# Weights-stationary products as three 256-column matmuls in one PSUM half instead of 512 + 256 columns joined afterwards

## Chip, cores, metric

One core of one Trainium2 chip. The metric is device time of one execution in microseconds, median of the runs.

## What is computed

Four post-norm residual layers on x of 256 tokens x 2048 features, float32: gated linear attention (GLA), a gated ConvFFN, a 2-D neighbourhood attention with relative position bias, and a second ConvFFN.

```python
def reference(x, ...):
    for i in range(DEPTH):                     # DEPTH = 2
        m = _gla_mixer(x, ...) if i % 2 == 0 else _na_mixer(x, ...)
        x = _layer_norm(DEEPNORM_ALPHA * x + m, ...)
        f = _conv_ffn(x, ffn_w_up[i], ffn_conv_w[i], ffn_conv_b[i], ffn_w_down[i])
        x = _layer_norm(DEEPNORM_ALPHA * x + f, ...)
    return x

def _conv_ffn(x, w_up, conv_w, conv_b, w_down):
    h = x @ w_up                               # 2048 -> 2 x 5632
    hp = jnp.pad(h, ((0, 0), (1, 1), (0, 0)))
    h = hp[:, :-2] * conv_w[0] + hp[:, 1:-1] * conv_w[1] + hp[:, 2:] * conv_w[2] + conv_b
    a, b = jnp.split(h, 2, axis=-1)
    return (jax.nn.gelu(a, approximate=False) * b) @ w_down
```

GLA projects x to q, k (1024 columns each), v, a gate g (2048 each) and a low-rank decay gate; the attention projects to q, k, v of 2048 each, 16 heads of 128.

## The kernel before

**Precision.** Every float32 operand is split into a high part (rounded to the type fp32r) and a low part, the rest (`emit_split`, lines 129 to 131: a ScalarE cast, a VectorE subtraction). A product is hi·hi + hi·lo + lo·hi. The activations xT and gT lie transposed in SBUF as tiles of 128 features with axes (k tile, token half t, part h, 128 tokens), where h = 0 is the high part and h = 1 the low one.

**Weights.** They come from HBM in units of 128 x 2048 floats (1 MB), in the order of `unit_plan`. `pump` (line 133) loads three units ahead (`raw`, DMA from the SyncE queue) and splits up to NS = 4 units ahead of the one in use into `hi` and `lo`, two pieces of 1024 columns each. `take` gives the next unit, `finish` frees one and calls `pump`.

**Two ways to multiply.** `as_block` (line 218) keeps activations stationary and streams 512 weight columns, for v, g and all output and down projections: three matmuls per k tile and token half. The weights-stationary way is used for q and k of GLA (16 units), q and k of the attention (32 units) and the up-projections (168 units), 216 units in all: `ws_one` (line 203) takes a unit of 128 output features, 16 k tiles, and `ws_part` (line 195) does two matmuls for each,

```python
mm(ps, hi3[:, kc], xs[:, kc].rearrange("p t h n -> p (t h n)"), kc == 0, False)
mm(ps4[:, :, 0], lo3[:, kc], xs[:, kc, :, 0], False, kc == KC - 1)
```

the first streams both parts of x (512 columns: for each token half 128 of the high part, then 128 of the low part) into a whole PSUM bank, the second streams the high parts alone (256 columns) with the low weights. The bank then holds two sums, of which the one over low parts has to be added: `join` (line 498) copies the odd quarter blocks to SBUF on ScalarE (line 502) and adds on VectorE (line 503). Each matmul has its own weight load of 128 columns. The first three units are done by the start-up code, which calls `ws_part` itself for three units side by side (line 449), and `low_rank` (line 480) has its own copy of the two lines.

**After the join.** In GLA the result goes to q or k. In the attention `qk_out` (line 747) splits it once more. In the FFN `conv` (line 673) multiplies by the middle tap and adds the bias on GpSimd (line 684), adds the two outer taps on VectorE (lines 685, 686), then comes Gelu on ScalarE (697) for the first half, or the product (702) and a split into gT for the second. Eight pieces of the FFN come from transposes instead and take the branch `joined`, whose middle tap is a ScalarE activation that reads PSUM (line 682).

**Order.** Work off the main line (scores, softmax, layer norms) is queued with `later` and let in by `tick` between groups of four k tiles. Each engine runs its own instructions in order. PSUM has five banks for `ps_mm` and three for `ps_tp`.

Of the kernel before, what the change touches and what calls it, by code (L numbers as in the profile page):

```python
# [10 lines left out]
F32 = mybir.dt.float32  # L11
F32R = mybir.dt.float32r
I32 = mybir.dt.int32
AF = mybir.ActivationFunctionType
ALU = mybir.AluOpType
AX = mybir.AxisListType

P = 128
D = 2048
T = 256  # L20
KC = D // P
# [16 lines left out]
NCT = FF // P  # L38
# [38 lines left out]
def kernel(  # L77
# [16 lines left out]
    nc = tc.nc  # L94
# [14 lines left out]
    def ps_mm():  # L109
        return psum.tile([P, 512], F32, tag="mm", name="ps_mm", bufs=8 - TP)  # L110

    def ps_tp():
        return psum.tile([P, 512], F32, tag="tp", name="ps_tp", bufs=TP)
# [15 lines left out]
    def emit_split(src, hi, lo):  # L129
        nc.scalar.copy(hi, src)  # L130
        nc.vector.tensor_tensor(lo, src, hi.bitcast(F32), ALU.subtract)  # L131
# [27 lines left out]
    def take():  # L159

        pump()
        j = st["next"]
        st["next"] = j + 1
        return splits.pop(j)

    def finish():
        st["done"] += 1
        pump()
# [3 lines left out]
    def later(fn, delay=1, chain=True):  # L172

        now = st["tick"]
        due = delay + (max([now] + [d for d, _ in side[-1:]]) if chain else now)
        side.append((due, fn))
        side.sort(key=lambda i: i[0])

    def tick():
        st["tick"] += 1  # L180
        while side and side[0][0] <= st["tick"]:
            side.pop(0)[1]()

        if slow and slow[0][0] <= st["tick"]:
            slow.pop(0)[1]()
# [5 lines left out]
    def mm(o, l, r, start, stop):  # L191
        nc.tensor.matmul(o, l, r, start=start, stop=stop)  # L192


    def ws_part(xs, hi, lo, ps, kcs):
        hi3 = hi.rearrange("p (k m) -> p k m", m=P)
        lo3 = lo.rearrange("p (k m) -> p k m", m=P)
        ps4 = ps.rearrange("p (t h n) -> p t h n", t=2, h=2)
        for kc in kcs:
            mm(ps, hi3[:, kc], xs[:, kc].rearrange("p t h n -> p (t h n)"), kc == 0, False)  # L200
            mm(ps4[:, :, 0], lo3[:, kc], xs[:, kc, :, 0], False, kc == KC - 1)

    def ws_one(xs, evac):
        hi, lo = take()
        ps = ps_mm()
        for c in range(4):
            ws_part(xs, hi, lo, ps, range(4 * c, 4 * c + 4))
            tick()
        evac(ps)
        finish()  # L210

# [57 lines left out]
    xT = act.tile([P, KC, 2, 2, P], F32R, tag="xT", name="xT")  # L269
# [87 lines left out]
    def load_g(pool, idx):  # L357
        g = pool.tile([P, D], F32, tag="gb", name="g")
        nc.gpsimd.dma_start(g, lnp[idx, 0:1, :].broadcast_to([P, D]))
        return g  # L360

    def load_gb(pool, idx):
        b = pool.tile([P, D], F32, tag="b", name="b")
        nc.gpsimd.dma_start(b, lnp[idx, 1:2, :].broadcast_to([P, D]))
        return load_g(scope["xp"], idx), b
# [32 lines left out]
    def open_pool(name):  # L398
        scope["pool"] = scope["stack"].enter_context(tc.tile_pool(name=name, bufs=1))
        return scope["pool"]  # L400
# [7 lines left out]
    gla = open_pool("gla")  # L408
# [43 lines left out]
    hi = hi_p.tile([P, 2048], F32R, tag="hi", name="hi")  # L452
    lo = lo_p.tile([P, 2048], F32R, tag="lo", name="lo")
# [44 lines left out]
    def join(pool, dst, ps):  # L498

        ps4 = ps.rearrange("p (t h n) -> p t h n", t=2, h=2)  # L500
        tmp = pool.tile([P, 2, P], F32, tag="join", name="join_t", bufs=2)
        nc.scalar.copy(tmp, ps4[:, :, 1])  # L502
        nc.vector.tensor_tensor(dst.rearrange("p (t n) -> p t n", t=2), ps4[:, :, 0], tmp, ALU.add)  # L503

    def gla_head(h):
        q = gla.tile([P, 2, T], F32, tag="q", name="q")
        k = gla.tile([P, 2, T], F32, tag="k", name="k")
# [122 lines left out]
        if h == 0:  # L630
            for c in range(2):
                join(gla, q[:, c], first_ps[c])
                finish()
            join(gla, k[:, 0], first_ps[2])
            finish()
            ws_one(xT, lambda ps: join(gla, k[:, 1], ps))
            low_rank()
        later(gate_weights, 0)
        later(lambda: gates(0), 4 if h == 0 else 2)
        later(lambda: gates(1), 3)  # L640
        if h > 0:
            for c in range(2):
                ws_one(xT, lambda ps: join(gla, q[:, c], ps))
            for c in range(2):
                ws_one(xT, lambda ps: join(gla, k[:, c], ps))
        later(lambda: decay(0), 1)
        later(lambda: decay(1), 4)
        later(scores, 6)
# [16 lines left out]
    def ffn(layer):  # L665
        pool = scope["pool"]
        idx = 2 * layer + 1
        cw = pool.tile([P, 2 * NCT, 3], F32, name="cw")
        nc.gpsimd.dma_start(cw, convw[:, layer])
        cb = pool.tile([P, 2 * NCT], F32, name="cb")  # L670
        nc.gpsimd.dma_start(cb, convb[:, layer])

        def conv(i, ch, ps, joined=False):
            if joined:
                hh = ps
            else:
                hh = pool.tile([P, T], F32, tag="h", name="h", bufs=3)
                join(pool, hh, ps)
            c = pool.tile([P, T], F32, tag=f"c{i}", name="c", bufs=2)
            w_ = cw[:, ch]  # L680
            if joined:
                nc.scalar.activation(c, hh, AF.Identity, bias=cb[:, ch:ch + 1], scale=w_[:, 1:2])
            else:
                nc.gpsimd.tensor_scalar(c, hh, w_[:, 1:2], cb[:, ch:ch + 1], ALU.mult, ALU.add)  # L684
            nc.vector.scalar_tensor_tensor(c[:, 1:], hh[:, :T - 1], w_[:, 0:1], c[:, 1:], ALU.mult, ALU.add)  # L685
            nc.vector.scalar_tensor_tensor(c[:, :T - 1], hh[:, 1:], w_[:, 2:3], c[:, :T - 1], ALU.mult, ALU.add)  # L686
            return c

        for part, (c0, n) in enumerate(THIRDS):
            held = {}  # L690

            def evac(i, ps, joined=False):
                kc = i // 2
                if i % 2 == 0:
                    c = conv(0, c0 + kc, ps, joined)
                    ge = pool.tile([P, T], F32, tag="ge", name="ge", bufs=2)
                    nc.scalar.activation(ge, c, AF.Gelu)  # L697
                    held["a"] = ge
                else:
                    c = conv(1, NCT + c0 + kc, ps, joined)  # L700
                    gg = pool.tile([P, T], F32, tag="gg", name="gg", bufs=2)
                    nc.vector.tensor_tensor(gg, held["a"], c, ALU.mult)  # L702
                    emit_split(gg.rearrange("p (t n) -> p t n", t=2), gT[:, kc, :, 0], gT[:, kc, :, 1])

            start = 0
            if part == 0:

                ht = {}

                def h_out(t, ps):  # L710
                    ht[t] = pool.tile([P, 512], F32, tag="ht", name="ht", bufs=2)
                    nc.scalar.copy(ht[t], ps)

                def pair(i):
                    tp = ps_tp()
                    for j in range(2):
                        for t in range(2):
                            nc.tensor.transpose(tp[:, j * T + t * P:j * T + t * P + P],
                                                ht[t][:, (2 * j + i) * P:(2 * j + i) * P + P], ident)
                    for j in range(2):  # L720
                        evac(2 * i + j, tp[:, j * T:j * T + T], True)

                as_block(xT, 4, h_out, apart=True, settle=True)
                later(lambda: pair(0), 1)
                later(lambda: pair(1), 1)
                start = 4
            for i in range(start, 2 * n):
                ws_one(xT, lambda ps: evac(i, ps))
            if part == 0:
                scope["gb"] = load_gb(pool, idx) if idx == 2 * DEPTH - 1 else load_g(scope["xp"], idx)  # L730
            residual_out(gT, part == 0, part == len(THIRDS) - 1, n // 4, idx)


    def attention():
# [3 lines left out]
        def head(h):  # L738
            pool = scope["pool"]
            q = pool.tile([P, 2, T], F32R, tag="q", name="q", bufs=2)  # L740
            k = pool.tile([P, 2, T], F32R, tag="k", name="k", bufs=2)
# [3 lines left out]
            v = vt[h // 4]  # L745
            hv = slice((h % 4) * P, (h % 4) * P + P)
            def qk_out(dst, ps):
                f = pool.tile([P, T], F32, tag="qk", name="qk", bufs=1)
                join(pool, f, ps)
                emit_split(f, dst[:, 0], dst[:, 1])  # L750
            ws_one(xT, lambda ps: qk_out(q, ps))
            ws_one(xT, lambda ps: qk_out(k, ps))
            cell = {}

            def score():
# [62 lines left out]
    for h in range(HG):  # L818
        gla_head(h)
# [15 lines left out]

    residual_out(gT, True, True, 4, 0, begin_gla_out)
    ffn(0)
    attention()
    residual_out(gT, True, True, 4, 2, begin_na_out)
# [75 lines left out]
```

## Time and profile before

| | |
|---|---|
| median of 3 runs | 2282.26 us (2282.12 to 2282.65) |
| profiled execution | 2282.44 us |
| its span | 2280.6 us |
| matmuls, weight loads | 11740 each |
| TensorE matmul busy | 2262.1 us (99%) |
| VectorE, ScalarE, GpSimd busy | 1506.3, 1056.7, 317.7 us |

PE is the matmul part of TensorE and PEld its weight loads, which are recorded apart and overlap matmuls; DVE is VectorE, ACT ScalarE, POOL GpSimd. The recorded duration of a matmul runs from its start to the modelled end of its last column, so durations of neighbours overlap; how fast matmuls follow each other is read from their starts in the timeline. A group of instructions is a line, an engine, an operation and the tiles that it writes and reads.

### The profile page before, as it was taken

The page shows a single profiled execution, that of the slowest core. Times are in us where ns is not written, and L with a number is a line of the kernel's source. Part 1 is how long each engine was busy: PE and PEld are TensorE (multiplying, and loading weights), DVE is VectorE, ACT ScalarE, POOL GpSimd, SP SyncE. Part 2 cuts the span into 40 slices and gives each one's busy share as a digit, 9 for nine tenths or more (in the row PEclk, how much of TensorE's full clock was granted, in tenths as well). Part 3 has the DMA queues.
Part 4 walks back from the last instruction along what each step waited for, and adds up shares of the span by engine and source line. Part 5 has one row for each costly group of instructions (what it writes and reads, how often), then busy time and mean ns, then how long its engine had stood idle before and what let it go on. Part 6 is the DMA issues. An engine that isn't in the chain of part 4 may idle for free. (4 is left out here: it accounts for less than half of the span.)

```text
span 2280.6 us, 29636 instructions
## 1 busy us (share of the span) xinstructions
PE 2262.1 (99%) x11740; PEld 1925.1 (84%) x11740; DVE 1506.3 (66%) x2096; ACT 1056.7 (46%) x1537; POOL 317.7 (14%) x272
## 2 busy tenths in 40 slices
PE   9999999999999999999999999999999999999997
PEld 7888888888888888888888888888888888888886
DVE  7656656866656665676686666667676567756775
ACT  6654544544434444344464555446444444434442
POOL 1101000222002220122010100001220022201211
PEclk9999999999999999999999999999999999999999
DMA  8544464745554445555585555547446555565452
GB/s 279 187 168 169 182 243 157 250 184 185 203 188 181 185 178 209 186 184 185 185 258 187 194 189 198 202 165 240 176 176 227 195 175 179 183 216 188 174 198 93
DMA packets 66602, 439.02 MB, mean 193 GB/s; under 512 B 7648, under 2 KB 9952, under 8 KB 15136
## 3 DMA queue, kind: packets, MB, share of 16 engines
q1 hardware_dynamic: 60336, 415.00, 50.1%
q0 software_dynamic: 5840, 21.61, 3.8%
q8 instruction: 92, 1.51, 0.3%
q10 hardware_dynamic: 288, 0.52, 0.1%
q14 instruction: 46, 0.38, 0.0%
HBM read 431.87 MB, written 2.10 MB: 190 GB/s over the span
## 5 line engine op out<-in xcount | busy, mean ns | idle before, releaser
L131 DVE TENSOR_TENSOR lo<-raw,hi 128x1024 fp32r<-128x1024 f32 (+1 forms) x791 | 943.2, 1210 | 486.6 <-ACT hi L130 485.6
L192 PE MATMUL ps_mm<-xT,hi 128*128 128x512 f32 x3472 | 1229.3, 399 | 2.4 <-ACT hi L130 1.8
L130 ACT CAST hi<-raw 128x1024 fp32r<-128x1024 f32 (+1 forms) x791 | 806.7, 1041 | 514.3 <-PE ps_mm L192 485.1
L192 PE MATMUL ps_mm<-xT,lo 128*128 128x256 f32 x3472 | 974.5, 281 | 0.2 <-DVE lo L131 0.2
L192 PEld LDWEIGHTS ps_mm<-xT,hi 128*128 128x128 f32 x3472 | 651.7, 188 | 162.6 <-ACT hi L130 2.6
L192 PEld LDWEIGHTS ps_mm<-xT,lo 128*128 128x128 f32 x3472 | 655.3, 189 | 1.5 <-DVE lo L131 0.8
L192 PE MATMUL ps_mm<-hi,gT 128*128 128x512 f32 x1920 | 594.6, 390 | 0.0
L192 PEld LDWEIGHTS ps_mm<-hi,gT 128*128 128x128 f32 x1920 | 360.2, 188 | 74.5
L684 POOL TENSOR_SCALAR c<-h,cw,cb 128x256 f32<-128x256 f32 x168 | 239.0, 1422 | 1070.2 <-DVE h L503 1070.2
L192 PE MATMUL ps_mm<-lo,gT 128*128 128x512 f32 x960 | 373.5, 389 | 0.0
L192 PE MATMUL ps_mm<-hi,xT 128*128 128x512 f32 x896 | 284.1, 391 | 0.4 <-DVE xT L131 0.4
L192 PEld LDWEIGHTS ps_mm<-lo,gT 128*128 128x128 f32 x960 | 180.2, 188 | 37.2
L192 PEld LDWEIGHTS ps_mm<-hi,xT 128*128 128x128 f32 x896 | 167.9, 188 | 35.6 <-DVE xT L131 1.2
L192 PE MATMUL ps_mm<-lo,xT 128*128 128x512 f32 x448 | 174.8, 390 | 0.0
L130 ACT CAST gT<-gg 128x256 fp32r<-128x256 f32 x88 | 35.6, 407 | 285.4 <-DVE gg L702 285.4
L697 ACT ACTIVATE ge<-c 128x256 f32<-128x256 f32 x88 | 36.7, 417 | 251.4 <-DVE c L686 251.3
L685 DVE SCALAR_TENSOR_TENSOR c<-h,cw,c 128x255 f32<-128x255 f32 x168 | 81.3, 484 | 76.3 <-POOL c L684 76.3
L192 PEld LDWEIGHTS ps_mm<-lo,xT 128*128 128x128 f32 x448 | 84.2, 188 | 17.4 <-DVE rs_m L276 0.7
L686 DVE SCALAR_TENSOR_TENSOR c<-h,cw,c 128x255 f32<-128x255 f32 x168 | 81.3, 484 | 5.9
L502 ACT COPY join_t<-ps_mm 128x256 f32<-128x256 f32 x216 | 78.3, 363 | 1.8 <-issue 1.0
L503 DVE TENSOR_TENSOR h<-ps_mm,join_t 128x256 f32<-128x256 f32 x168 | 70.2, 418 | 5.2 <-ACT join_t L502 5.2
L131 DVE TENSOR_TENSOR gT<-gg,gT 128x256 fp32r<-128x256 f32 x88 | 37.7, 430 | 38.8 <-ACT gT L130 38.8
(139 smaller groups left out, 784.2 us busy)
## 6 DMA issues: line engine op xcount, KB each, us to landing
raw<-in_w_dram SPq DMA_DIRECT2D x388, 1024.0 KB, 4.8
x_sb<-in_lnp_dram POOLq DMA_DIRECT2D x6, 1024.0 KB, 10.6
g<-in_lnp_dram POOLq DMA_DIRECT2D x4, 1024.0 KB, 15.9
raw<-in_w_dram SPq DMA_DIRECT2D x12, 256.0 KB, 6.9
bt<-in_bias_dram POOLq DMA_DIRECT2D x16, 192.0 KB, 2.9
bt<-bmask_sb POOLq DMA_DIRECT2D x16, 192.0 KB, 3.1
xr<-in_xt_dram SPq DMA_DIRECT2D x8, 256.0 KB, 5.7
x_sb<-in_x_dram POOLq DMA_DIRECT2D x1, 2048.0 KB, 9.6
```

What stands on the lines that cost most here:

```text
L130: nc.scalar.copy(hi, src)
L131: nc.vector.tensor_tensor(lo, src, hi.bitcast(F32), ALU.subtract)
L192: nc.tensor.matmul(o, l, r, start=start, stop=stop)
L502: nc.scalar.copy(tmp, ps4[:, :, 1])
L503: nc.vector.tensor_tensor(dst.rearrange("p (t n) -> p t n", t=2), ps4[:, :, 0], tmp, ALU.add)
L684: nc.gpsimd.tensor_scalar(c, hh, w_[:, 1:2], cb[:, ch:ch + 1], ALU.mult, ALU.add)
L685: nc.vector.scalar_tensor_tensor(c[:, 1:], hh[:, :T - 1], w_[:, 0:1], c[:, 1:], ALU.mult, ALU.add)
L686: nc.vector.scalar_tensor_tensor(c[:, :T - 1], hh[:, 1:], w_[:, 2:3], c[:, :T - 1], ALU.mult, ALU.add)
L697: nc.scalar.activation(ge, c, AF.Gelu)
```

## The change

`ws_one` becomes `ws_half`. It uses half a PSUM bank, 256 columns, and does three matmuls of 256 columns for each k tile, all summed into the same place: high weights on the high parts of x, high weights on the low parts, low weights on the high parts. There is nothing to join then, and each user of the result reads PSUM directly: GLA copies it with ScalarE, the attention splits it from PSUM, and the FFN's `conv` takes the branch that was there for the transposed pieces, with the middle tap on ScalarE and the two outer taps on VectorE reading PSUM. `tick` is called after the same k tiles. The three start-up units, `low_rank` and `as_block` stay.

```diff
--- before.py
+++ after.py
@@ -200,12 +200,18 @@
             mm(ps, hi3[:, kc], xs[:, kc].rearrange("p t h n -> p (t h n)"), kc == 0, False)
             mm(ps4[:, :, 0], lo3[:, kc], xs[:, kc, :, 0], False, kc == KC - 1)
 
-    def ws_one(xs, evac):
+    def ws_half(xs, evac):
+
         hi, lo = take()
-        ps = ps_mm()
-        for c in range(4):
-            ws_part(xs, hi, lo, ps, range(4 * c, 4 * c + 4))
-            tick()
+        ps = ps_mm()[:, :T]
+        hi3 = hi.rearrange("p (k m) -> p k m", m=P)
+        lo3 = lo.rearrange("p (k m) -> p k m", m=P)
+        for kc in range(KC):
+            mm(ps, hi3[:, kc], xs[:, kc, :, 0], kc == 0, False)
+            mm(ps, hi3[:, kc], xs[:, kc, :, 1], False, False)
+            mm(ps, lo3[:, kc], xs[:, kc, :, 0], False, kc == KC - 1)
+            if kc % 4 == 3:
+                tick()
         evac(ps)
         finish()
 
@@ -633,16 +639,16 @@
                 finish()
             join(gla, k[:, 0], first_ps[2])
             finish()
-            ws_one(xT, lambda ps: join(gla, k[:, 1], ps))
+            ws_half(xT, lambda ps: nc.scalar.copy(k[:, 1], ps))
             low_rank()
         later(gate_weights, 0)
         later(lambda: gates(0), 4 if h == 0 else 2)
         later(lambda: gates(1), 3)
         if h > 0:
             for c in range(2):
-                ws_one(xT, lambda ps: join(gla, q[:, c], ps))
+                ws_half(xT, lambda ps: nc.scalar.copy(q[:, c], ps))
             for c in range(2):
-                ws_one(xT, lambda ps: join(gla, k[:, c], ps))
+                ws_half(xT, lambda ps: nc.scalar.copy(k[:, c], ps))
         later(lambda: decay(0), 1)
         later(lambda: decay(1), 4)
         later(scores, 6)
@@ -670,18 +676,10 @@
         cb = pool.tile([P, 2 * NCT], F32, name="cb")
         nc.gpsimd.dma_start(cb, convb[:, layer])
 
-        def conv(i, ch, ps, joined=False):
-            if joined:
-                hh = ps
-            else:
-                hh = pool.tile([P, T], F32, tag="h", name="h", bufs=3)
-                join(pool, hh, ps)
+        def conv(i, ch, hh):
             c = pool.tile([P, T], F32, tag=f"c{i}", name="c", bufs=2)
             w_ = cw[:, ch]
-            if joined:
-                nc.scalar.activation(c, hh, AF.Identity, bias=cb[:, ch:ch + 1], scale=w_[:, 1:2])
-            else:
-                nc.gpsimd.tensor_scalar(c, hh, w_[:, 1:2], cb[:, ch:ch + 1], ALU.mult, ALU.add)
+            nc.scalar.activation(c, hh, AF.Identity, bias=cb[:, ch:ch + 1], scale=w_[:, 1:2])
             nc.vector.scalar_tensor_tensor(c[:, 1:], hh[:, :T - 1], w_[:, 0:1], c[:, 1:], ALU.mult, ALU.add)
             nc.vector.scalar_tensor_tensor(c[:, :T - 1], hh[:, 1:], w_[:, 2:3], c[:, :T - 1], ALU.mult, ALU.add)
             return c
@@ -689,15 +687,15 @@
         for part, (c0, n) in enumerate(THIRDS):
             held = {}
 
-            def evac(i, ps, joined=False):
+            def evac(i, ps):
                 kc = i // 2
                 if i % 2 == 0:
-                    c = conv(0, c0 + kc, ps, joined)
+                    c = conv(0, c0 + kc, ps)
                     ge = pool.tile([P, T], F32, tag="ge", name="ge", bufs=2)
                     nc.scalar.activation(ge, c, AF.Gelu)
                     held["a"] = ge
                 else:
-                    c = conv(1, NCT + c0 + kc, ps, joined)
+                    c = conv(1, NCT + c0 + kc, ps)
                     gg = pool.tile([P, T], F32, tag="gg", name="gg", bufs=2)
                     nc.vector.tensor_tensor(gg, held["a"], c, ALU.mult)
                     emit_split(gg.rearrange("p (t n) -> p t n", t=2), gT[:, kc, :, 0], gT[:, kc, :, 1])
@@ -718,14 +716,14 @@
                             nc.tensor.transpose(tp[:, j * T + t * P:j * T + t * P + P],
                                                 ht[t][:, (2 * j + i) * P:(2 * j + i) * P + P], ident)
                     for j in range(2):
-                        evac(2 * i + j, tp[:, j * T:j * T + T], True)
+                        evac(2 * i + j, tp[:, j * T:j * T + T])
 
                 as_block(xT, 4, h_out, apart=True, settle=True)
                 later(lambda: pair(0), 1)
                 later(lambda: pair(1), 1)
                 start = 4
             for i in range(start, 2 * n):
-                ws_one(xT, lambda ps: evac(i, ps))
+                ws_half(xT, lambda ps: evac(i, ps))
             if part == 0:
                 scope["gb"] = load_gb(pool, idx) if idx == 2 * DEPTH - 1 else load_g(scope["xp"], idx)
             residual_out(gT, part == 0, part == len(THIRDS) - 1, n // 4, idx)
@@ -745,11 +743,9 @@
             v = vt[h // 4]
             hv = slice((h % 4) * P, (h % 4) * P + P)
             def qk_out(dst, ps):
-                f = pool.tile([P, T], F32, tag="qk", name="qk", bufs=1)
-                join(pool, f, ps)
-                emit_split(f, dst[:, 0], dst[:, 1])
-            ws_one(xT, lambda ps: qk_out(q, ps))
-            ws_one(xT, lambda ps: qk_out(k, ps))
+                emit_split(ps, dst[:, 0], dst[:, 1])
+            ws_half(xT, lambda ps: qk_out(q, ps))
+            ws_half(xT, lambda ps: qk_out(k, ps))
             cell = {}
 
             def score():
```

On TensorE, in the attention where the scores of a head (`ps_tp<-k,q`) stand between k tiles of the next projection (`x6` is six equal matmuls in a row), before:

```order
L192 MATMUL ps_mm<-xT,hi 128x512
L192 MATMUL ps_mm<-xT,lo 128x2x128
L192 MATMUL ps_tp<-k,q 128x256 x6
L192 MATMUL ps_mm<-xT,hi 128x512
L192 MATMUL ps_mm<-xT,lo 128x2x128
```

and after the change:

```order
L192 MATMUL ps_mm<-xT,hi 128x256 x2
L192 MATMUL ps_mm<-xT,lo 128x256
L192 MATMUL ps_tp<-k,q 128x256 x6
L192 MATMUL ps_mm<-xT,hi 128x256 x2
L192 MATMUL ps_mm<-xT,lo 128x256
```

The places are the same; each 512-column matmul is two of 256 now, and the output of the third (128x2x128 before, two runs of 128) is one run.

On VectorE, in the up-projection of a later pair of units (c is the convolution's sum, h the joined tile, gg the gated product, lo the low part of weights to come), before:

```order
L131 TENSOR_TENSOR lo<-raw,hi 128x1024
L685 SCALAR_TENSOR_TENSOR c<-h,cw,c 128x255
L686 SCALAR_TENSOR_TENSOR c<-h,cw,c 128x255
L702 TENSOR_TENSOR gg<-ge,c 128x256
L131 TENSOR_TENSOR gT<-gg,gT 128x2x128
L131 TENSOR_TENSOR lo<-raw,hi 128x1024
L503 TENSOR_TENSOR h<-ps_mm,join_t 128x256
L131 TENSOR_TENSOR lo<-raw,hi 128x1024
```

and after the change:

```order
L683 SCALAR_TENSOR_TENSOR c<-ps_mm,cw,c 128x255
L131 TENSOR_TENSOR lo<-raw,hi 128x1024
L684 SCALAR_TENSOR_TENSOR c<-ps_mm,cw,c 128x255
L700 TENSOR_TENSOR gg<-ge,c 128x256
L131 TENSOR_TENSOR gT<-gg,gT 128x2x128
L131 TENSOR_TENSOR lo<-raw,hi 128x1024
L683 SCALAR_TENSOR_TENSOR c<-ps_mm,cw,c 128x255
L131 TENSOR_TENSOR lo<-raw,hi 128x1024
```

The addition that writes h is gone, the outer taps read ps_mm, and a split of weights stands between the two taps that followed each other before.

## Rows read from the trace of the kernel before

**Rows 1.** The page, parts 1 and 2: engines busy, granted clock per slice.
```profile
PE 2262.1 (99%) x11740; PEld 1925.1 (84%) x11740; DVE 1506.3 (66%) x2096; ACT 1056.7 (46%) x1537; POOL 317.7 (14%) x272
...
PEclk9999999999999999999999999999999999999999
```

**Rows 2.** Waits of TensorE (PE) and its weight loads (PEld), whole span: total, times, longest.
```profile
PE ps_mm L192 <- ACT hi L130: 1.8, 2, 0.9
...
PEld ps_tp L301 <- DVE ln_f L311: 3.1, 5, 0.9
```

**Rows 3.** Line 192 in 667.1 to 847: min/median/max, first and last start.
```profile
L192 PE MATMUL ps_mm<-xT,hi x510: 389/398/403, 667.0 to 846.9; 128*128 128x512 f32 x170
```

**Rows 4.** Timeline of TensorE in the up-projection: start, duration, instruction.
```profile
500.08 0.40 PE L192 MATMUL ps_mm<-xT,hi 128*128 128x512 f32 x1
...
501.14 0.40 PE L192 MATMUL ps_mm<-xT,hi 128*128 128x512 f32 x1
```

**Rows 5.** Timeline of TensorE in the GLA stage.
```profile
101.26 0.39 PE L192 MATMUL ps_mm<-xT,hi 128*128 128x512 f32 x1
...
102.30 0.39 PE L192 MATMUL ps_mm<-xT,hi 128*128 128x512 f32 x1
```

**Rows 6.** Timeline of TensorE in an activation-stationary block.
```profile
1304.45 0.39 PE L192 MATMUL ps_mm<-lo,xT 128*128 128x512 f32 x1
...
1305.13 0.39 PE L192 MATMUL ps_mm<-lo,xT 128*128 128x512 f32 x1
```

**Rows 7.** Groups by line and form, TensorE, activation-stationary: count, busy us, mean ns.
```profile
L192 PE MATMUL ps_mm<-hi,gT 128*128 128x512 f32 x1920 | 594.6, 390 | 0.0
...
L192 PEld LDWEIGHTS ps_mm<-hi,gT 128*128 128x128 f32 x1920 | 360.2, 188 | 74.5
```

**Rows 8.** Timeline of TensorE around the scores of an attention head.
```profile
1192.40 0.87 PE L192 MATMUL ps_tp<-k,q 128*128 128x256 f32 x6
1193.11 0.39 PE L192 MATMUL ps_mm<-xT,hi 128*128 128x512 f32 x1
```

**Rows 9.** Timeline of TensorE around the products with v, two heads.
```profile
1263.19 0.86 PE L192 MATMUL ps_tp<-pt,v 128*128 128x256 f32 x6
1263.88 0.39 PE L192 MATMUL ps_mm<-xT,hi 128*128 128x512 f32 x1
...
1302.15 0.87 PE L192 MATMUL ps_tp<-pt,v 128*128 128x256 f32 x6
1302.86 0.39 PE L192 MATMUL ps_mm<-hi,xT 128*128 128x512 f32 x1
```

**Rows 10.** Line 192 in 1218.7 to 1219.2, then in 1263.5 to 1263.85.
```profile
L192 PE MATMUL ps_tp<-k,q x6: 278/283/283, 1218.5 to 1219.1; 128*128 128x256 f32 x6
...
L192 PE MATMUL ps_tp<-pt,v x5: 276/276/281, 1263.3 to 1263.8; 128*128 128x256 f32 x5
```

**Rows 11.** Groups by line and form: the evacuation on ScalarE, VectorE and GpSimd.
```profile
L684 POOL TENSOR_SCALAR c<-h,cw,cb 128x256 f32<-128x256 f32 x168 | 239.0, 1422 | 1070.2 <-DVE h L503 1070.2
...
L502 ACT COPY join_t<-ps_mm 128x256 f32<-128x256 f32 x216 | 78.3, 363 | 1.8 <-issue 1.0 <-PE ps_mm L192 0.8
L503 DVE TENSOR_TENSOR h<-ps_mm,join_t 128x256 f32<-128x256 f32 x168 | 70.2, 418 | 5.2 <-ACT join_t L502 5.2
...
L682 ACT ACTIVATE c<-ps_tp,cb,cw 128x256 f32<-128x256 f32 x8 | 4.5, 557 | 0.5 <-PE ps_tp L718 0.3
...
L686 DVE SCALAR_TENSOR_TENSOR c<-ps_tp,cw,c 128x255 f32<-128x255 f32 x8 | 3.8, 480 | 0.1
```

**Rows 12.** Busy us in 667.1 to 847: PE, PEld, DVE, ACT, POOL, then the clock.
```profile
667.10:847.00 179.90, 179.90 (x1020) 156.11 (x1019) 124.58 (x182) 79.04 (x121) 42.71 (x30) 1.00 0.47 181
```

**Rows 13.** Timeline of TensorE behind a wait, in the first layer's down-projection.
```profile
391.79 0.66 PE L301 MATMUL ps_tp<-ident,x_sb 128*128 128x128 f32 x4 [0.48 <-DVE ln_f L311]
392.20 0.71 PE L192 MATMUL ps_mm<-hi,gT 128*128 128x512 f32 x2
```

## The prediction

> **What bounds the kernel now.** The median of the three runs is 2282.26 us; the profiled execution took 2282.44 us, of which 2280.6 us are the span, so a sum made on the span carries over to the median by adding 1.7 us. I call a difference measurable here when it is over 0.2%, that is 4.6 us.
>
> I read the page's first part first. TensorE's matmuls cover 99% of the span, at the full granted clock (tens, not halves, in every slice: its 2.4 GHz level), VectorE 66%, ScalarE 46%, GpSimd 14% [rows 1]. A covered span alone does not say that TensorE is at its peak, since matmuls overlap in the record, so the waits come next: the largest entry in TensorE's own list is 1.8 us, and that of its weight loads 3.1 us [rows 2]. Nothing feeds TensorE late. The time of this kernel is therefore the number of its instructions times the distance from one start to the next, and the whole question is what that distance becomes.
>
> The third view gives the distance in the stage that the change touches. In the second part of the first layer's up-projection, 510 matmuls of 512 columns, each followed by its partner of 256, start between 667.0 and 846.9 us [rows 3]: 179.9 / 509 = **353.4 ns for one pair**. The timeline shows the same over three pairs, 500.08 to 501.14, 1.06 us [rows 4]. In the GLA stage the pair is a little shorter: 101.26 to 102.30 holds three, 346.7 ns each [rows 5]. The activation-stationary blocks, where each matmul has 512 columns, start three of them between 1304.45 and 1305.13, 226.7 ns apart [rows 6], with a weight load of 188 ns that fits beneath [rows 7]. Their records are about 162 ns longer than that distance (0.39 us less 0.227), a fixed latency, so that for other shapes too a duration less 162 is roughly the pace.
>
> **The change, part by part.** (1) *TensorE.* Of 216 weights-stationary units the first three stay as they are (the start-up code calls ws_part itself), so 213 units of 16 steps change: 3408 steps. A step now streams 512 + 256 columns and loads weights twice; after the change it streams 256 three times and loads three times. The columns are the same 768. What is added is one matmul and one weight load per step. The load of the same weights a second time is not left out by anything: in the activation-stationary blocks the first two of every three matmuls have the same stationary tile in a row, and the rows count 1920 loads for 1920 matmuls [rows 7].
>
> So I need the pace of back-to-back 256-column matmuls with one load each. The kernel has such runs, six long. The scores of the attention are even the same pattern, twice q's high part and then its low part: 1192.40 to the next start at 1193.11 [rows 8], 0.71 / 6 = 118.3 ns. The products with v give 0.71 us for six for one head and 0.69 us for another (115.0 ns) [rows 9]. That is 345 to 355 ns for three. I take 118 ns, the value of the runs nearest in pattern, so **354 ns for a step** against 353.4. Inside those runs the pace drifts, which sets the outer bounds: where another head's scores have records of 283 ns in the median the pace is 283 - 162 = 121 ns, taken as 120, or 360 a step; where the products with v settle at 276 ns it is 276 - 162 = 114 ns, and half of the 512-column distance, 113.4, is the floor, or 340 a step [rows 6, 10].
>
> Sum for TensorE: 3200 steps outside GLA by +0.6 ns = +1.9 us, and 208 in GLA (13 units) by +7 ns = +1.5 us; together +3.4 us. Bounds over all 3408: 340 gives -13.4 ns, -46 us; 360 gives +6.6 ns, +22 us.
>
> The rows show a load of 188 ns lying under a matmul whose next start is 227 ns away, and in runs of 256 columns six loads that overlap their neighbours, so an added load does not stand alone. The Trainium skill, TensorE: Matmul & The Clock Gate, section Part 3: Packing small matmuls, says that a weight load overlaps a running matmul only if it goes to another row group (another section of the page allows the spare weight buffer); here every load takes all rows, and by that rule each added load would stand in the open, 3408 x 188 ns = +641 us. The trace disagrees, with 118 ns per matmul and load together.
>
> (2) *Evacuation.* The ScalarE copy of 363 ns and the VectorE add of 418 ns go from all but three of 216 units. In the FFN GpSimd's multiply of 1422 ns goes too, 168 of them, and ScalarE does it from PSUM instead at 557 ns, the price of the eight that it did already; VectorE's two taps stay and read PSUM, where a tap of those eight pieces costs 480 ns [rows 11]. Per unit VectorE loses 0.42 us, ScalarE gains 0.19, GpSimd is emptied. In the attention one copy and one add per unit vanish; in GLA one add. None of this is on the path: in the 179.9 us that I measured the pair in, VectorE was busy 124.58 us and ScalarE 79.04 [rows 12], so both have room. I cost it at nothing; the cover is TensorE itself, whose list of waits names these engines with a few microseconds in the whole run [rows 2].
>
> (3) *Order.* On VectorE the two taps, which stood side by side behind GpSimd, are now parted by a split of weights, and on TensorE nothing moves. The accumulator's bank is now held until the second tap, some 557 + 2 x 480 ns and a split between them, estimated from its 1024 columns against the tap's 255 and 480 ns as at most 1.9 us: 3.4 us in all, and ScalarE's activation stands at the place of the old copy, waiting for the same last matmul, with the next splits queued behind it as before. A unit takes 16 x 354 = 5.7 us and there are five banks, so a bank is wanted again after some 28 us, and the splits run up to four units ahead. Nothing comes due.
>
> Total 2282.4 + 3.4 - 0.2 (profiled to median) = 2285.6; I say **2285 us**, no measurable change.
>
> **Rivals.**
> *Faster pace (36%).* A long uniform stream could settle at 114 ns, as the products with v do after three matmuls, instead of 118. Against it: most runs of six don't. All steps at 113.4 give 2282.3 - 46 = 2236 us; half of the way 2259.
> *Slower pace (24%).* The score pattern, hi hi lo, is exactly the new one, and once settles at about 120 ns [rows 10]. If that is the steady state: 2282.3 + 22 = 2304 us. It decides from 119 ns on (357 a step, +12 us). This rival ends on the other side of the forecast, by nothing but the steady state of loads and matmuls.
> *Issue of instructions (6%).* TensorE must now take six instructions in the time of four. Runs of six could be fed from what was issued ahead during the slower stretches; a stream of 3072 matmuls could not. From 59 ns an instruction on (354 / 6) this sets the pace. Against it: right behind a wait of 0.48 us four transposes and their loads take 391.79 to 392.20, 51 ns an instruction [rows 13]. Proven for long stretches is only the present 353.4 / 4 = 88 ns, which would make a step 530 ns and the time 2884 us, as the far end; between 59 and 88 the time is open. The Trainium skill, same page, section Wait — 56ns, not 53.3ns?, gives 62 ns a matmul where the sequencer's own program decodes it; if loads cost the same, an estimate from that page is 372 ns a step, +63 us; no run of before decides which way it decodes.
> *A new wait (4%).* VectorE reads PSUM twice per FFN unit and holds the bank longer. Should a bank be late by the whole hold of 3.4 us in each of 168 units, the time is +570 us; it decides only from a hold of about four units, 22 us. The profile speaks against it with VectorE idle for 34% of the span.
>
> **Numbers.** The forecast's own case, 352 to 355 ns a step, has 30%, and its own range is 2277 to 2289. Cases by sign: faster by over 0.2% is the faster rival and 1% of the forecast's edge, 0.37; within 0.2% (2277.7 to 2286.8) 0.25; slower is the slower pace 24, issue 6, new wait 4 and 4 of the forecast's edge, 0.38. The range takes in both ends of the pace with 2 us to spare above, 2236 to 2306, and leaves out issue, the new wait and a little of the tails.
>
> **What would show it.** In the profile after: TensorE's matmuls x15148, each with its load, still at the full clock; in the second part of the up-projection 1536 starts of 256 columns 118 ns apart, so 181.2 us for its 512 steps, which take 180.9 now; waits of TensorE still of a few us; GpSimd near 3%; VectorE busy some 90 us less. The forecast is wrong if records of these matmuls are 276 ns (faster) or 283 (slower) instead of 280, or if TensorE's list names an accumulator's reader.

## Result and the profile after

The changed kernel takes 2306.18 us (median of 4 runs, 2305.95 to 2306.34) against 2282.45 us: ratio 1.0104, 95% interval 1.0091 to 1.0117. It is slower by 23.7 us, just beyond the upper end of the range. The profiled execution took 2306.34 us with a span of 2304.6 us. Ratios here and below compare runs at the full granted clock; one run of the last experiment (hi lo lo hi), at a mean clock of 0.85, took 2466.91 us and is left out.

The page after, the lines that answer to [rows 1]:

```profile
PE 2286.6 (99%) x15148; PEld 2107.8 (91%) x15148; DVE 1409.1 (61%) x1883; ACT 1093.0 (47%) x1505; POOL 77.1 (3%) x104
...
PEclk9999999999999999999999999999999999999999
```

VectorE lost 97 us and GpSimd 241, the clock is unchanged, and matmuls and loads rose by 3408 each. TensorE waits no more than before; its two lists of waits (TensorE, then its loads) begin, where [rows 2] stood, with

```profile
PE ps_tp L307 <- DVE ln_f L317: 1.5, 3, 0.6
...
PEld ps_tp L307 <- DVE ln_f L317: 3.1, 5, 1.0
```

So the time is in the pace. The second part of the first up-projection, as in [rows 3], by the view of line 192 (min/median/max, then first and last start), in 672.3 to 856:

```profile
L192 PE MATMUL ps_mm<-xT,hi x1022: 278/283/283, 672.2 to 856.0; 128*128 128x256 f32 x171
L192 PEld LDWEIGHTS ps_mm<-xT,hi x1021: 188/192/192, 672.2 to 855.8; 128*128 128x128 f32 x171
...
L192 PE MATMUL ps_mm<-xT,lo x510: 283/283/283, 672.5 to 855.7; 128*128 128x256 f32 x170
```

One low-part matmul per step: (855.7 - 672.5) / 509 = 359.9 ns a step, where [rows 3] gave 353.4, and 120.0 ns a matmul. The shortest and the median record of the low-part matmuls are equal, 283 ns: nothing here varies. In the trace of before, the scores of one head shown in [rows 10] had this median. The timeline in this stage shows the same three times in a row (start, duration; x2 is two high-part matmuls):

```profile
760.07 0.40 PE L192 MATMUL ps_mm<-xT,hi 128*128 128x256 f32 x2
760.31 0.28 PE L192 MATMUL ps_mm<-xT,lo 128*128 128x256 f32 x1
760.43 0.40 PE L192 MATMUL ps_mm<-xT,hi 128*128 128x256 f32 x2
760.67 0.28 PE L192 MATMUL ps_mm<-xT,lo 128*128 128x256 f32 x1
760.79 0.40 PE L192 MATMUL ps_mm<-xT,hi 128*128 128x256 f32 x2
```

The sum closes: 3200 steps by 6.6 ns are 21.1 us, the 208 of GLA by 360 - 347 = 13 ns [rows 5] are 2.7 us, together 23.8 of the measured 23.7 us.

The trace after shows why runs of six had misled. Behind six products with v, the projection starts faster than it goes on (each line is the start of a step; nine matmuls lie between two of them):

```profile
1201.20 0.39 PE L192 MATMUL ps_mm<-xT,hi 128*128 128x256 f32 x2
...
1202.26 0.40 PE L192 MATMUL ps_mm<-xT,hi 128*128 128x256 f32 x2
...
1203.34 0.40 PE L192 MATMUL ps_mm<-xT,hi 128*128 128x256 f32 x2
```

The first nine take 1.06 us, 118 ns each, the next nine 1.08 us, 120 ns each. Behind a block of 512-column matmuls the first nine take 1.08 us at once:

```profile
672.24 0.40 PE L192 MATMUL ps_mm<-xT,hi 128*128 128x256 f32 x2
...
673.32 0.40 PE L192 MATMUL ps_mm<-xT,hi 128*128 128x256 f32 x2
```

So the pace of a short run depends on what stands before it. The kernel before has runs of the second kind too: in four of the sixteen heads the scores stand between 512-column matmuls, and all four have a median of 283 ns. One is in [rows 10], another is

```profile
L192 PE MATMUL ps_tp<-k,q x6: 278/283/283, 1292.8 to 1293.4; 128*128 128x256 f32 x6
```

### The profile page after: what moved, and what is told of

Its sections match the earlier page's. It is cut to its first block, busy times and chain, and to the rows that moved or that the text cites. A ratio compares the mean times of both kernels' runs of the same rounds, so it can differ in the third digit from the quotient of the medians.

```text
span 2304.6 us, 35893 instructions
## 1 busy us (share of the span) xinstructions
PE 2286.6 (99%) x15148; PEld 2107.8 (91%) x15148; DVE 1409.1 (61%) x1883; ACT 1093.0 (47%) x1505; POOL 77.1 (3%) x104
## 5 line engine op out<-in xcount | busy, mean ns | idle before, releaser
L192 PE MATMUL ps_mm<-xT,hi 128*128 128x256 f32 (+1 forms) x6880 | 1253.8, 284 | 1.8 <-ACT hi L130 1.3
L192 PEld LDWEIGHTS ps_mm<-xT,hi 128*128 128x128 f32 x6880 | 1075.3, 192 | 7.4 <-ACT hi L130 2.3
L192 PEld LDWEIGHTS ps_mm<-xT,lo 128*128 128x128 f32 x3472 | 665.6, 192 | 0.7 <-DVE lo L131 0.5
L682 ACT ACTIVATE c<-ps_mm,cb,cw 128x256 f32<-128x256 f32 x168 | 94.4, 562 | 0.0
L683 DVE SCALAR_TENSOR_TENSOR c<-ps_mm,cw,c 128x255 f32<-128x255 f32 x168 | 80.0, 476 | 0.3 <-ACT c L682 0.3
L684 DVE SCALAR_TENSOR_TENSOR c<-ps_mm,cw,c 128x255 f32<-128x255 f32 x168 | 80.0, 476 | 0.0
L283 POOL TENSOR_TENSOR ln_rs<-rs_m,mhalf 128x1 f32<-128x1 f32 x8 | 7.1, 888 | 1617.0 <-DVE rs_m L282 1617.0
L387 DVE SCALAR_TENSOR_TENSOR x_sb<-x_sb,ps_mm 128x512 f32<-128x512 f32 x32 | 21.9, 687 | 31.8 <-PE ps_mm L192 31.8
```

The source lines that it names most:

```text
L283: nc.gpsimd.tensor_tensor(dst, m, mhalf, ALU.pow)
L387: nc.vector.scalar_tensor_tensor(blk, blk, ALPHA, ps, ALU.mult, ALU.add)
```

## Experiments

Theories before the first runs. **F**: every matmul with its own load costs its columns at 2.4 per ns and some 13.3 ns more, the line through the two measured paces (512: 213.3 + 13.3 = 226.7 [rows 6]; 256: 106.7 + 13.3 = 120), so three matmuls cost 360 and two at least 346.7. Rivals: **L**, back-to-back loads of 128 columns set the 120; **S**, adding three times in a row into the same PSUM columns; **R**, the new readers of PSUM; **P**, a cost in proportion to columns, 113.3 for 256, with a floor.

### Three matmuls, everything else as before

```diff
-        for c in range(4):
-            ws_part(xs, hi, lo, ps, range(4 * c, 4 * c + 4))
-            tick()
...
+        for kc in range(KC):
+            mm(ps4[:, :, 0], hi3[:, kc], xs[:, kc, :, 0], kc == 0, False)
+            mm(ps4[:, :, 1], hi3[:, kc], xs[:, kc, :, 1], False, False)
+            mm(ps4[:, :, 0], lo3[:, kc], xs[:, kc, :, 0], False, kc == KC - 1)
...
```

> This is the kernel before with its 512-column matmul cut into two of 256 that write the two interleaved parts of the bank, so that join, GpSimd and all the evacuation stay as they were. Theory F (a fixed cost: a matmul with its own load costs its columns at 2.4 per ns and 13.3 ns more, 226.7 ns for 512 and 120 for 256) and theory L (back-to-back loads of 128 columns set the 120 ns): the step goes from 353.4 to 360 ns as in the changed kernel, the time to 2305 us, 1.0%. Theory S (three matmuls in a row that add into the same 256 columns are what slows) and theory R (the readers of PSUM are): the step stays near 353 ns and the time within 0.2% of 2282 us.

Measured: 2306.3 us, ratio 1.0106 (1.0089 to 1.0123), the changed kernel's time to 0.1 us. The page's busy times:

```profile
PE 2285.6 (99%) x15148; PEld 2107.0 (91%) x15148; DVE 1507.6 (65%) x2096; ACT 1057.3 (46%) x1537; POOL 317.3 (14%) x272
```

Line 192 in 672.3 to 856:

```profile
L192 PE MATMUL ps_mm<-xT,hi x1022: 277/283/283, 672.1 to 855.8; 128*128 128x256 f32 x171
```

VectorE, ScalarE and GpSimd do the old work, and TensorE keeps the new pace (283 ns). S and R fall: where the sums go and who reads them is worth nothing, in either direction. The whole loss is that of cutting one matmul in two.

### Wider matmuls

```diff
...
+                mv = xs[:, kc].rearrange("p t h n -> p (t h n)")[:, :width]
+                mm(ps, hi3[:, kc], mv, kc == 0, False)
+                mm(ps, hi3[:, kc], mv, False, False)
+                mm(ps, lo3[:, kc], mv, False, kc == KC - 1)
...
```

> The changed kernel, with the three matmuls of an up-projection step streaming 256, 320, 384 columns in the three parts of the first FFN and 416, 448, 512 in those of the second, all with the same loads; the products are not the reference's. Theory F: 120, 146.7, 173.3, 186.7, 200 and 226.7 ns from start to start. Theory P (cost in proportion to columns, 226.7 ns per 512, with a floor of 120 from the loads): 120, 141.7, 170, 184.2, 198.4 and 226.7 ns.

Line 192 in one window of each of the six parts:

```profile
L192 PE MATMUL ps_mm<-xT,lo x428: 283/283/283, 429.9 to 583.7; 128*128 128x256 f32 x143
...
L192 PE MATMUL ps_mm<-xT,lo x509: 309/309/309, 672.2 to 895.7; 128*128 128x320 f32 x170
...
L192 PE MATMUL ps_mm<-xT,lo x381: 334/334/343, 985.1 to 1182.8; 128*128 128x384 f32 x191
...
L192 PE MATMUL ps_mm<-xT,lo x438: 346/353/353, 1676.0 to 1922.9; 128*128 128x416 f32 x146
...
L192 PE MATMUL ps_mm<-xT,lo x511: 362/365/369, 2011.7 to 2321.8; 128*128 128x448 f32 x171
...
L192 PE MATMUL ps_mm<-xT,lo x383: 389/389/389, 2410.1 to 2669.9; 128*128 128x512 f32 x192
```

Last start less first, by the count less one, by three: 120.1, 146.7, 173.4, 188.3, 202.7 and 226.7 ns. F said 120, 146.7, 173.3, 186.7, 200, 226.7; P's 141.7 and 170 are out. From 256 to 512 columns the pace rises by 226.7 - 120.1 = 106.6 ns, which is 2.4 columns per ns. At widths from 320 on the pace is far above the 112 ns at which full loads follow each other in the next experiment, yet the 13.3 ns stay (15.0 at 416 columns, 16.0 at 448). They are a price per matmul with its load; no run has a matmul without one, so the two are not told apart. The first part also reads x in one run of 256 columns, where the changed kernel reads two of 128: its 120.1 ns rule that out as the reason.

### Narrower matmuls

```diff
...
+                full = xs[:, kc].rearrange("p t h n -> p (t h n)")
+                n = T if kc == 0 else width
+                mm(ps[:, :n], hi3[:, kc], full[:, :n], kc == 0, False)
+                mm(ps[:, :n], hi3[:, kc], full[:, :n], False, False)
+                mm(ps[:, :n], lo3[:, kc], full[:, :n], False, kc == KC - 1)
...
```

> The changed kernel, with the matmuls of an up-projection step (all but those of a unit's first k tile) streaming 64, 128, 160 columns in the three parts of the first FFN and 192, 224, 240 in those of the second, with unchanged loads of 128 columns; the rest of the products is left out. Theory F, if the fixed cost belongs to the matmul: 40, 66.7, 80, 93.3, 106.7 and 113.3 ns from start to start. Theory L: 120 ns in all six, or the 111.7 ns that float32 products of 128 columns show, down to some width. A floor between the two gives the price of a load by itself.

Line 192 in the parts with 64, 128 and 240 columns; then busy times of the first two (PE, PEld, DVE, ACT, POOL, then the granted clock):

```profile
L192 PE MATMUL ps_mm<-xT,lo x407: 401/401/415, 440.0 to 699.8; 128*128 128x64 f32 x128, 128*128 128x256 f32 x8
...
L192 PE MATMUL ps_mm<-xT,lo x477: 273/275/278, 799.9 to 959.8; 128*128 128x128 f32 x149, 128*128 128x256 f32 x10
...
L192 PE MATMUL ps_mm<-xT,lo x356: 272/274/280, 2170.1 to 2289.7; 128*128 128x240 f32 x178
```

```profile
440.00:700.00 260.00, 260.00 (x1220) 260.00 (x1221) 91.95 (x129) 71.92 (x102) 0.00 (x0) 0.50 0.30 107
800.00:960.00 160.00, 160.00 (x1432) 160.00 (x1431) 106.61 (x150) 84.67 (x119) 0.00 (x0) 1.00 0.55 194
```

From 128 to 240 columns the pace is the same: (959.8 - 799.9) / 476 / 3 = 112.0 ns and (2289.7 - 2170.1) / 355 / 3 = 112.3 ns (the three parts between lie within 112.1 to 112.9). That is a floor: neither F's 66.7 to 113.3 nor L's 120. In a stretch of full loads with their matmuls one pair takes 112 ns, however few columns stream, and 256 columns are only 8 ns above that. Most of the part of 64 columns ran at half the clock (0.50), 213 ns each, but its first 8 us ran at the full one:

```profile
426.88 0.28 PE L192 MATMUL ps_mm<-xT,lo 128*128 128x64 f32 x1
...
429.22 0.28 PE L192 MATMUL ps_mm<-xT,lo 128*128 128x64 f32 x1
```

Seven steps lie between these two, (429.22 - 426.88) / 21 = 111 ns each: the same floor. Since it nearly doubles, to 213 ns, at half of TensorE's clock, it goes with that clock. That it is the load's own, and not one that any matmul has, is argued and not shown, as all these matmuls had full loads.

### Shorter loads

```diff
...
+            m = P if kc in (0, KC - 1) else cols
+            mm(ps[:m], hi3[:, kc, :m], xs[:, kc, :, 0], kc == 0, False)
+            mm(ps[:m], hi3[:, kc, :m], xs[:, kc, :, 1], False, False)
+            mm(ps[:m], lo3[:, kc, :m], xs[:, kc, :, 0], False, kc == KC - 1)
...
```

> The changed kernel, with the weight loads of the up-projections cut to 32, 64, 96 columns in the three parts of the first FFN and 112, 120, 128 in those of the second (all k tiles of a unit but its first and last), while each matmul still streams 256 columns; the products for the other weight columns are left out. If the 13.3 ns belong to the matmul whatever it loads: 120 ns from start to start in all six parts. If they are the price of bringing in the loaded columns (13.3 ns per 128): 110, 113.3, 116.7, 118.3, 119.2 and 120 ns. If the load is the bound after all, the pace falls to 113 ns or less as soon as the load is a little shorter.

Line 192 in the parts with loads of 32, 64, 96, 112, 120 and 128 columns (128*64 is rows by loaded columns; two of sixteen k tiles keep full loads):

```profile
L192 PE MATMUL ps_mm<-xT,lo x428: 276/281/287, 429.8 to 578.7; 128*32 128x256 f32 x125, 128*128 128x256 f32 x18
...
L192 PE MATMUL ps_mm<-xT,lo x508: 276/276/283, 667.9 to 841.7; 128*64 128x256 f32 x150, 128*128 128x256 f32 x20
...
L192 PE MATMUL ps_mm<-xT,lo x382: 274/278/283, 929.8 to 1062.7; 128*96 128x256 f32 x167, 128*128 128x256 f32 x24
...
L192 PE MATMUL ps_mm<-xT,lo x432: 276/276/283, 1555.0 to 1702.7; 128*112 128x256 f32 x126, 128*128 128x256 f32 x18
...
L192 PE MATMUL ps_mm<-xT,lo x509: 277/279/283, 1791.8 to 1971.0; 128*120 128x256 f32 x149, 128*128 128x256 f32 x21
...
L192 PE MATMUL ps_mm<-xT,lo x379: 283/283/283, 2059.8 to 2195.9; 128*128 128x256 f32 x190
```

The same division gives 116.2, 114.3, 116.3, 114.2, 117.6 and 120.0 ns. The full load is the one case that stands fixed at 120 with a median of 283 ns; a load shorter by 16 columns brings most matmuls to 276 ns, the lowest value of [rows 10]. The third forecast comes nearest: with two of sixteen k tiles at 120, a mean of 114.2 means 113.4 elsewhere. So not all of the 13.3 ns at 256 columns belongs to the matmul alone: some 6 of them appear only beside a full load. But 32 and 96 columns are slower than 64, which none of the three allowed. F holds as a rule for full loads from 256 columns on, within 3 ns; how load and stream meet in detail stays open.

### The order of the old pair

```diff
...
+        if group == 0:
+            order = [(kc, part) for kc in range(KC) for part in ("hl", "lh")[kc % 2]]
+        else:
+            order = [(kc, part) for k0 in range(0, KC, group) for part in "hl" for kc in range(k0, k0 + group)]
...
```

> The kernel before, with the order of the two kinds of matmuls changed in the up-projections: groups of 1, 2 and 4 k tiles (first all of a group's 512-column matmuls, then its 256-column ones) in the parts of the first FFN; groups of 8, of 16, and hi lo lo hi in turn in those of the second. Theory F has a floor of 226.7 + 120 = 346.7 ns a step for every order, so the present 353.4 holds 6.7 ns of something else. If that something comes once for each passage from a 256-column matmul to a 512-column one: 353.4, 350.0, 348.4, 347.5, 347.1 and 350.0 ns. If it comes with each load that has only a 256-column matmul to lie under: 353.4 in all. Theory P (113.3 ns for 256 columns, 340 a step) leaves 13.4 of something else: 353.4, 346.7, 343.3, 341.7, 340.8, 346.7.

By F the old pair should cost 346.7 ns and took 353.4. The first starts of the projection and of the block behind it, in the timeline of the six parts, with groups of 1, 2, 4, 8, 16 and with hi lo lo hi:

```profile
423.57 0.48 PE L192 MATMUL ps_mm<-xT,hi 128*128 128x512 f32 x1
...
579.11 0.40 PE L192 MATMUL ps_mm<-hi,gT 128*128 128x512 f32 x1
...
666.22 0.62 PE L192 MATMUL ps_mm<-xT,hi 128*128 128x512 f32 x2
...
844.55 0.40 PE L192 MATMUL ps_mm<-hi,gT 128*128 128x512 f32 x1
...
931.60 0.62 PE L192 MATMUL ps_mm<-xT,hi 128*128 128x512 f32 x2
...
1066.29 0.40 PE L192 MATMUL ps_mm<-hi,gT 128*128 128x512 f32 x1
...
1552.29 0.94 PE L192 MATMUL ps_mm<-xT,hi 128*128 128x512 f32 x3
...
1706.01 0.40 PE L192 MATMUL ps_mm<-hi,gT 128*128 128x512 f32 x1
...
1793.08 1.30 PE L192 MATMUL ps_mm<-xT,hi 128*128 128x512 f32 x5
...
1971.19 0.40 PE L192 MATMUL ps_mm<-hi,gT 128*128 128x512 f32 x1
...
2058.25 0.39 PE L192 MATMUL ps_mm<-xT,hi 128*128 128x512 f32 x1
...
2192.01 0.39 PE L192 MATMUL ps_mm<-hi,gT 128*128 128x512 f32 x1
```

Over 440, 512, 384, 440, 512 and 384 steps: 353.5, 348.3, 350.8, 349.4, 347.9 and 348.3 ns. Groups of one are the old order and take the old time. The others are all below 353.4 and none is below 346.7, so P's 340.8 is out once more; but groups of four and of eight cost more than groups of two, so "once for each passage" is not the rule either. The whole mixture took 2271.39 us, 0.5% less than the kernel before (one run).

### A version that beats both

The kernel before with one order in all 213 units, hi lo lo hi in turn, or all sixteen high-part matmuls and then the sixteen others.

> The kernel before with only the order of its two matmuls changed in all 213 units: hi lo, lo hi in turn, so that two 512-column matmuls and two of 256 stand together. From the 348.2 ns a step that this order showed in one part of the up-projection against 353.4, theory F gives 3200 x -5.2 = -17 us outside GLA and a little back in GLA, where the step was 346.7 before: 2266 us, 0.7% faster than the kernel before and 1.7% faster than the changed one. If the gain in that part was an accident of its place, 2282.

> The kernel before with all sixteen 512-column matmuls of a unit first and then its sixteen of 256, in all 213 units. Theory F with the 348.0 ns a step of that part gives about -17 us, 2265 us; were the something else paid once for each passage between the kinds, this order, which has eight times fewer passages than the zigzag, would come to 347 ns and 2260 us.

Measured: 2266.79 us (three runs), ratio 0.9932 (0.9912 to 0.9951), and 2266.95 us (four runs), ratio 0.9931 (0.9917 to 0.9946), both against 2282.67 us of the kernel before. The timeline of the second shows the two prices side by side:

```profile
703.38 3.82 PE L192 MATMUL ps_mm<-xT,hi 128*128 128x512 f32 x16
707.03 2.08 PE L192 MATMUL ps_mm<-xT,lo 128*128 128x256 f32 x16
708.94 3.36 PE L192 MATMUL ps_mm<-xT,hi 128*128 128x512 f32 x14
```

3.65 / 16 = 228 ns for 512 columns, 1.91 / 16 = 119 ns for 256, 347.5 ns together. The gains of 15.9 and 15.7 us are nearly the 17 that F gave for both. Fewer passages bring no more, so the alternative in the last expectation, 2260 us, falls.

## Why the prediction was wrong

**What bounds the kernel** was right: TensorE alone, without waits, and a sum of starts. The whole 23.7 us is steps by pace.

**The pace of short matmuls** is the step that failed: "I take 118 ns, the value of the runs nearest in pattern, so 354 ns for a step". The value was read from runs of six that stand inside other work [rows 8, 9], where the first matmuls of a run still go by what stood before them: 118 ns each for the first nine behind products with v, 120 ns from then on. The projections after stand at 120 by the thousand, and so do runs behind 512-column matmuls from their second or third matmul on. The mechanism (a pace per matmul) was right and the term mis-sized: 360 instead of 354 per step, +21.1 us instead of +1.9 outside GLA, and +2.7 instead of +1.5 inside. The rows that showed it stood in the trace of before: records of 283 ns in the median [rows 10], in all four heads whose scores stand between 512-column matmuls, named as the slower rival (2304 us, 24%), which is what happened. The prediction took them for one exception; they were the runs least disturbed by what stood before. What should have moved the rival ahead is the sum 106.7 + 13.3, which puts 120 and the 226.7 of [rows 6] on one line; I called 162 ns of a record its latency and never asked what the columns alone would take. Of the 13.3 ns that a further matmul costs by F, GLA shows all (347 to 360) and the rest only 6.6, because there the old pair already took 6.7 ns more than the sum of its parts. The range's end, 2306, came from the same 120 ns and missed by 0.2 us, for GLA's pairs were counted at 353.4 in that bound although [rows 5] had them at 347.

**Evacuation at nothing** was right: the first experiment has the old evacuation and the same time to 0.1 us, and a PSUM bank held through both taps delayed nobody.

**The rivals.** The faster pace fell: 276 ns is not a steady state with full loads. Issue of instructions fell: the matmuls of 128 columns in the third experiment kept 112 ns for a load and a matmul, 56 ns an instruction, over a whole stage (in the trace of before 24 such pairs already ran so, between 63.49 and 66.08 us), so the estimate of 62 ns for each of both, made from the Trainium skill's TensorE: Matmul & The Clock Gate, section Wait — 56ns, not 53.3ns?, does not hold here. No new wait came. The rule on row groups that the Trainium skill gives in the same page, section Part 3: Packing small matmuls, stays contradicted: 3408 more loads, each with its matmul, cost 7 ns a step, not 188.

## What to carry to other kernels

Where TensorE is full, count matmuls with their loads and not columns alone: with a load of 128 columns each, these float32 matmuls cost about 13 ns beyond their columns, and cutting 512 into two of 256 cost 1% of the whole here, whatever work it saved on engines that have room. Read a pace from stretches as long as the one you forecast. If there are only short ones, look at what stands before each: the ends of two kinds of runs of six were 114 and 120 ns here [rows 10], and only the long stretch told which holds. Where matmuls of two lengths alternate, try putting equal ones together: here that alone was worth 0.7%.

## Not expected

With 64 columns each, narrow matmuls were slower in time, not only in worth: after 8 us of that stage at 112 ns the granted clock fell from 1.00 to 0.50 (its 1.2 GHz level), with TensorE's record busy without a gap, and the pace to 213 ns. It was back at 1.00 in the down-projection behind the stage:

```profile
423.50:430.50 7.00, 7.00 (x66) 7.00 (x65) 5.59 (x8) 5.57 (x8) 1.44 (x2) 1.00 1.00 328
431.60:703.50 271.90, 271.90 (x1277) 271.90 (x1276) 98.04 (x141) 77.43 (x110) 0.00 (x0) 0.50 0.32 115
708.00:740.00 32.00, 32.00 (x143) 26.45 (x142) 14.28 (x16) 11.65 (x13) 0.00 (x0) 1.00 0.53 185
```

That kernel took 2374.96 us although it computes less. The parts of 128 columns and more kept 1.00 throughout. It is one run, and that the narrow matmuls made the clock fall is suggested by where it fell and rose, not shown.

A weight load's record of 188 to 192 ns is not what a load costs in a stream: loads followed each other every 112 ns.

Open: why pairs of 512 and 256 take 353.4 ns in the up-projection and 346.7 in GLA with the same code, what fixes 120 ns beside a full load and 114 beside one of 64 or 112 columns, and whether the 13 ns would go with a matmul that needs no load of its own.
